# First row tile's attention scores by one 256-column matmul per component, in heads 0 to 5 of a decoder block

## The chip, the cores and the metric

The kernel runs on one core of a Trainium2 chip. The metric is the device time in microseconds (us) of one execution. A core has five engines with instruction queues of their own: PE (matmuls, with its weight loads shown as PEld), DVE (vector operations), ACT (activations and copies), POOL (GpSimd) and SP (which issues most of the transfers). Each queue runs in its own order, and engines wait for one another by semaphores.

## The reference

The block works on 512 rows of width 1024 in float32. Cut to the part around the change:

```python
h = rmsnorm(x, norm_attn_g)
u_q, u_k, u_v, u_pool, u_gate = split(h @ w_in)
# 8 heads, 2 components of 64 dimensions each, values 128 wide
for i in range(S // Q_BLOCK):                 # row tiles of 128
    s = einsum('bqhcd,bkhcd->bhcqk', q[:, q0:kend], k[:, :kend])
    s = where(mask, s, -inf)                  # causal
    p = softmax(s, axis=-1)
    w = p[:, :, 0] - lam * p[:, :, 1]         # difference of the two components
    outs.append(einsum('bhqk,bkhd->bqhd', w, v[:, :kend]))
a = rmsnorm(o, subln_g) * (1 - lam_init)
merged = sigmoid(g_A) * a + sigmoid(g_P) * pool(u_pool)
x = x + merged @ w_out
x = x + relu(rmsnorm(x) @ w_up)**2 @ w_down
```

Queries carry a factor of 1/8, and a rotary embedding turns 16 of the 64 dimensions of queries and keys.

## The kernel before

Precision is kept by splitting operands into a high part in float32r (a reduced float32 format of the matmul) and a low part, the rest. A projection is 24 matmuls of 512 columns: high by high, high by low, low by high (lines 131, 132, 135). For the scores both parts of the query lie one above the other in the 128 partitions: tile `qs` holds, for component 0, the high part in partitions 0 to 63 and the low part in 64 to 127, and the other way round for component 1. The keys are in two tiles. `kz` has the high part against the query's high part and zeros in the other half. `ks` has the low part against the query's high part, and the high part against the query's low part. So a score tile is the sum of two matmuls into one PSUM bank, query by `ks` (line 395, which starts the sum) and query by `kz` (line 396, which ends it), with the same stationary `qs`.

For each head `attn` goes through four row tiles i = 0 to 3 with N = 128(i+1) key columns, and two components c in each. Per tile and component there are the two matmuls of N columns; one DVE reduction (line 397), which adds the causal mask, writes the negated scaled scores to `pr` and takes their row minimum into `st`; and one exponential on ACT (line 401). Then the tile's two components are joined (lines 403 to 406), transposed by PE against the identity (line 410, i+1 transposes), and split into high and low by ACT and DVE (412, 413). After the fourth tile twelve matmuls (line 418) multiply by the values.

Score banks come from a rotation of two, `sbk` = banks 3 and 4: before, each component of a tile takes the next one. Transposes rotate over banks 5 and 6, projections and the merge (lines 485 to 489) over 0 to 2, and bank 7 holds the head's output.

The head loop writes `attn(h)`, the next head's query and key projections `qk(h+1)`, and fillers (a pooling group's projection, or a gate's) up to a count in the table `LAG`. This isn't the order in which engines run. The tile framework's scheduler, with a timeline of its own, interleaves the instructions of these pieces on each engine when the program is built. So an edit of a few instructions gives another order in the whole attention stage. Transfers and all stages outside attention keep their code.

Of the kernel before, what the change touches and what calls it, by code (L numbers as in the profile page):

```python
# [18 lines left out]
P = 128  # L19
# [32 lines left out]
def block_kernel(ctx, tc, xT, x_tok, gains, pos, consts, w_in, w_v, w_pool, w_out, w_up, w_dn, out):  # L52
# [37 lines left out]
    def f(ap):  # L90
        return ap.bitcast(F32)
# [270 lines left out]

    lo_, hi_ = slice(0, 64), slice(64, 128)

    kzs = [cf.tile([P, 2, S], F32R, name=f"kz{i}") for i in range(2)]
    for kz in kzs:
        G.memset(f(kz)[hi_, 0, :], 0.0)
        G.memset(f(kz)[lo_, 1, :], 0.0)

    def qk(h):  # L370
        qs = tp.tile([P, 2, S], F32R, tag="qs", name=f"qs{h}", bufs=2)
        ks = tp.tile([P, 2, S], F32R, tag="ks", name=f"ks{h}", bufs=2)
        kz = kzs[h % 2]
        q = rope(proj(h, f"q{h}", V) if h else q0, f"q{h}")
        for c, own, oth in ((0, lo_, hi_), (1, hi_, lo_)):
            A.copy(out=qs[own, c, :], in_=q[own])
            V.tensor_tensor(out=qs[oth, c, :], in0=q[own], in1=f(qs)[own, c, :], op=ALU.subtract)
        k = rope(proj(8 + h, f"k{h}", V), f"k{h}")
        for c, own, oth in ((0, lo_, hi_), (1, hi_, lo_)):
            A.copy(out=kz[own, c, :], in_=k[own])  # L380
        for c, own, oth in ((0, lo_, hi_), (1, hi_, lo_)):
            A.copy(out=ks[oth, c, :], in_=f(kz)[own, c, :])
            V.tensor_tensor(out=ks[own, c, :], in0=k[own], in1=f(kz)[own, c, :], op=ALU.subtract)
        return qs, ks, kz

    def attn(h, qs, ks, kz):
        wt = wt_all
        for i in range(NT):
            N = (i + 1) * P
            qsl = slice(i * P, i * P + P)  # L390
            pr = tmp(f"p{i}", f"p{h}_{i}", (P, 2, N), bufs=1)
            st = tmp("st", f"st{h}_{i}", (P, 6), bufs=3)
            for c in range(2):
                s_ = sbk(f"s{h}_{i}_{c}")
                T.matmul(s_[:, :N], lhsT=qs[:, c, qsl], rhs=ks[:, c, :N], start=True, stop=False)
                T.matmul(s_[:, :N], lhsT=qs[:, c, qsl], rhs=kz[:, c, :N], start=False, stop=True)  # L396
                V.tensor_tensor_reduce(  # L397
                    out=pr[:, c, :N], in0=s_[:, :N], in1=mask[:, S - N :], scale=-0.125, scalar=-NEG,
                    op0=ALU.add, op1=ALU.min, accum_out=st[:, c : c + 1],
                )  # L400
                A.activation(out=pr[:, c, :N], in_=pr[:, c, :N], func=AF.Exp, scale=-1.0,  # L401
                             bias=st[:, c : c + 1], accum_out=st[:, 2 + c : 3 + c])
            V.reciprocal(out=st[:, 4:6], in_=st[:, 2:4])
            V.tensor_scalar(out=st[:, 5:6], in0=st[:, 5:6], scalar1=lvec, scalar2=None, op0=ALU.mult)
            A.activation(out=pr[:, 1, :N], in_=pr[:, 1, :N], func=AF.Copy, scale=st[:, 5:6])
            V.scalar_tensor_tensor(out=pr[:, 0, :N], in0=pr[:, 0, :N], scalar=st[:, 4:5], in1=pr[:, 1, :N],
                                   op0=ALU.mult, op1=ALU.add)
            t_ = tbk(f"t{h}_{i}")
            for j in range(i + 1):
                T.transpose(out=t_[:, j * P : j * P + P], in_=pr[:, 0, j * P : j * P + P], identity=ident)  # L410
            tv = t_[:, :N].rearrange("p (j q) -> p j q", q=P)
            A.copy(out=wt[:, 0, : i + 1, qsl], in_=tv)
            V.tensor_tensor(out=wt[:, 1, : i + 1, qsl], in0=tv, in1=f(wt)[:, 0, : i + 1, qsl], op=ALU.subtract)
        o_ = obk(f"o{h}")
        n = 0
        for vv, ww in ((vh, 0), (vl, 0), (vh, 1)):
            for j in range(NT):
                T.matmul(o_[:, j * P :], lhsT=vv[:, h, j * P : j * P + P], rhs=wt[:, ww, j, j * P :], start=n == 0, stop=n == 11,  # L418
                         skip_group_check=True)
                n += 1  # L420
        o = tmp("o", f"o{h}", bufs=2)
        A.copy(out=o, in_=o_)
        sqh = tmp("sqh", f"sqh{h}", dt=F32R, bufs=1)
        A.activation(out=sqh, in_=o_, func=AF.Square)
        sql = tmp("y", f"sql{h}", dt=F32R, bufs=1)
        sq = tmp("sq", f"sqo{h}")
        (V if h == H - 1 else G).tensor_tensor(out=sq, in0=o, in1=o, op=ALU.mult)
        (V if h == H - 1 else G).tensor_tensor(out=sql, in0=sq, in1=f(sqh), op=ALU.subtract)
        ss = obk(f"ss{h}")
        T.matmul(ss, lhsT=onesr, rhs=sqh, start=True, stop=False)  # L430
        T.matmul(ss, lhsT=onesr, rhs=sql, start=False, stop=True)
        y = tmp("y", f"y{h}", bufs=1)
        rsqrt(y, ss, sq, P)
        if h == H - 1:
            return o, y
        V.scalar_tensor_tensor(out=o, in0=o, scalar=subc, in1=y, op0=ALU.mult, op1=ALU.mult)
        return o, None
# [594 lines left out]
```

## Time and profile before

| | us |
|---|---|
| median of three runs (674.47 to 674.83) | 674.77 |
| the profiled execution's own time | 674.09 |
| its span, first to last instruction | 671.9 |
| PE busy | 663.1 (99%) |
| weight loads (beside PE) | 579.6 (86%) |
| DVE busy | 526.1 (78%) |
| ACT busy | 461.0 (69%) |
| POOL busy | 112.0 (17%) |

The mean granted PE clock was 0.996. The profiled execution's time is 2.19 us above its span, and 0.68 us below the median of the runs. Attention, with the projections and the merges that run among it, fills about 70 to 300 us of the span. In timelines the columns are start in us, duration in us, engine, line, operation, output and inputs, shapes, and a count; an entry in brackets is the idle time ahead of the instruction and what ended it. A matmul's duration reaches from its start until it leaves the array, and the next starts long before that; what a matmul costs PE is the step from its start to the next one's.

### The profile page before, as it was taken

What the parts mean: (1) busy time and instruction counts of PE and PEld (TensorE: products, weight loads), DVE (VectorE), ACT (ScalarE), POOL (GpSimd) and SP (SyncE); (2) the same over time, 40 slices, a digit from 0 to 9 for tenths busy, and PEclk for the clock granted to TensorE, in tenths of its full rate; (3) what the DMA queues carried; (4) which work ended last, traced back from release to release, by engine and by line L of the source; (5) the groups of instructions that cost most, each with busy time, mean ns of one, the idle gap of its engine ahead of it and who ended that gap; (6) DMA issues with size and microseconds to landing.
All of it is one profiled execution on the core that took longest, in us unless ns stands there. A gap on an engine that the chain in (4) does not pass through costs nothing.

```text
span 671.9 us, 9994 instructions
## 1 busy us (share of the span) xinstructions
PE 663.1 (99%) x3688; PEld 579.6 (86%) x3688; DVE 526.1 (78%) x882; ACT 461.0 (69%) x741; POOL 112.0 (17%) x130
## 2 busy tenths in 40 slices
PE   9999999999999999999999999999999999999995
PEld 7888888888888888888889988999889998899884
DVE  6855977799979986875588998657994599747995
ACT  8465587978887698884477975367743695256974
POOL 2001110142133212520202020202102021210120
PEclk9999999999999999999999999999999999999998
DMA  9416464435263365574976596776959578494863
GB/s 317 162 57 185 126 151 126 103 94 126 87 142 103 98 166 105 126 184 172 312 208 112 159 235 186 167 191 146 236 199 187 193 164 261 117 212 132 214 126 125
DMA packets 32880, 109.34 MB, mean 163 GB/s; under 512 B 4032, under 2 KB 4928, under 8 KB 32832
## 3 DMA queue, kind: packets, MB, share of 16 engines
q0 software_dynamic: 10656, 38.80, 32.3%
q1 hardware_dynamic: 21744, 69.38, 29.3%
q8 instruction: 29, 0.48, 0.3%
q10 hardware_dynamic: 432, 0.52, 0.2%
q14 instruction: 19, 0.16, 0.1%
HBM read 106.59 MB, written 2.10 MB: 162 GB/s over the span
## 4 chain that ended last, share of the span: by engine, by line
PE 98%; DMA 1%; DVE 0%; ACT 0%; issue 0%; SPq 0%
PE um L785 8%; PE um L788 8%; PE um L782 8%; PE dm L875 8%; PE dm L877 8%; PE dm L878 8%; PE v L235 2%; PE o L418 2%; PE ga L132 2%; PE ga L131 2%; PE gp L135 2%; PE gp L132 2%; PE k L132 2%; PE k L131 2%; PE gp L131 2%; PE k L135 2%
## 5 line engine op out<-in xcount | busy, mean ns | idle before, releaser
L877 PE MATMUL dm<-wh_dt,z 128*128 128x512 f32 (+1 forms) x128 | 49.5, 386 | 0.0
L878 PE MATMUL dm<-wl_dt,z 128*128 128x512 f32 (+1 forms) x128 | 49.4, 386 | 0.0
L875 PE MATMUL dm<-wh_dt,z 128*128 128x512 f32 (+1 forms) x128 | 49.0, 387 | 0.0
L785 PE MATMUL um<-gss,wh_ut 128*128 128x256 f32 x192 | 48.2, 283 | 0.0
L782 PE MATMUL um<-gss,wh_ut 128*128 128x256 f32 x192 | 48.0, 283 | 0.0
L401 ACT ACTIVATE p<-p,st 128x128 f32<-128x128 f32 (+3 forms) x64 | 35.7, 558 | 14.1 <-DVE st L397 13.8
L895 DVE TENSOR_TENSOR x<-x,dm 128x512 f32<-128x512 f32 x48 | 32.5, 681 | 16.3 <-PE dm L878 16.3
L112 ACT CAST wh_ut<-wga_uNone 128x1024 fp32r<-128x1024 f32 x24 | 24.9, 1050 | 29.7 <-PE dm L877 19.2
L112 ACT CAST wh_ub<-wr_u 128x1024 fp32r<-128x1024 f32 x24 | 25.1, 1050 | 22.1 <-PE um L785 9.8
L686 POOL DMA_DIRECT2D wga_dNone<-w_dn x16 | 14.2, 885 | 154.2 <-DVE wl_dt L113 154.2
L113 DVE TENSOR_TENSOR wl_ut<-wga_uNone,wh_ut 128x1024 fp32r<-128x1024 f32 x24 | 29.1, 1221 | 13.0 <-ACT wh_ut L112 12.9
L877 PE MATMUL dm<-wh_db,z 128*128 128x512 f32 x96 | 37.2, 389 | 0.0
L878 PE MATMUL dm<-wl_db,z 128*128 128x512 f32 x96 | 37.2, 389 | 0.0
L785 PEld LDWEIGHTS um<-gss,wh_ut 128*128 128x128 f32 x192 | 36.9, 192 | 0.0
L782 PEld LDWEIGHTS um<-gss,wh_ut 128*128 128x128 f32 x192 | 36.8, 192 | 0.0
L875 PE MATMUL dm<-wh_db,z 128*128 128x512 f32 x96 | 35.7, 389 | 0.0
L113 DVE TENSOR_TENSOR wl_ub<-wr_u,wh_ub 128x1024 fp32r<-128x1024 f32 x24 | 29.1, 1219 | 7.4 <-ACT wh_ub L112 7.4
L686 POOL DMA_DIRECT2D wga_uNone<-w_up x18 | 15.6, 865 | 115.8 <-DVE wl_ut L113 81.4
L112 ACT CAST wh_dt<-wga_dNone 128x1024 fp32r<-128x1024 f32 x24 | 24.9, 1049 | 14.4 <-issue 6.7
L755 DVE TENSOR_TENSOR z<-rawz,z 128x1024 fp32r<-128x1024 f32 x28 | 33.6, 1218 | 0.5 <-ACT z L752 0.5
L397 DVE CUSTOM_DVE_ANT_0 p<-s,mask 128x128 f32<-128x128 f32 (+3 forms) x64 | 30.3, 484 | 3.6 <-PE s L396 3.5
L785 PE MATMUL um<-gab,wh_ub 128*128 128x256 f32 x128 | 32.5, 283 | 0.0
(324 smaller groups left out, 2203.3 us busy)
## 6 DMA issues: line engine op xcount, KB each, us to landing
wr_u<-w_up SPq DMA_DIRECT2D x24, 512.0 KB, 5.4
wr_d<-w_dn SPq DMA_DIRECT2D x24, 512.0 KB, 4.2
wga_uNone<-w_up POOLq DMA_DIRECT2D x18, 512.0 KB, 7.2
wga_dNone<-w_dn POOLq DMA_DIRECT2D x16, 512.0 KB, 5.7
wr_k<-w_in SPq DMA_DIRECT2D x8, 512.0 KB, 3.3
wr_ga<-w_in SPq DMA_DIRECT2D x8, 512.0 KB, 3.3
wr_gp<-w_in SPq DMA_DIRECT2D x8, 512.0 KB, 4.2
wl_ga<-w_in POOLq DMA_DIRECT2D x8, 512.0 KB, 5.4
```

The source lines that it names most:

```text
L112: ins = A.copy(out=hi[:, sl], in_=raw[:, sl])
L113: (eng or G).tensor_tensor(out=lo[:, sl], in0=raw[:, sl], in1=f(hi)[:, sl], op=ALU.subtract)
L131: T.matmul(acc, lhsT=hi[:, c], rhs=rh[:, k, :], start=k == 0, stop=False)
L132: T.matmul(acc, lhsT=hi[:, c], rhs=rl[k], start=False, stop=False)
L401: A.activation(out=pr[:, c, :N], in_=pr[:, c, :N], func=AF.Exp, scale=-1.0, bias=st[:, c : c + 1], accum_out=st[:, 2 + c : 3 + c])
L755: lo = V.tensor_tensor(out=z[:, 1], in0=r, in1=f(z[:, 0]), op=ALU.subtract)
L782: m = T.matmul(a_, lhsT=hi[:, c], rhs=rh[:, k, :], start=p + k == 0 and onto is None, stop=False, skip_group_check=True)
L785: T.matmul(a_, lhsT=hi[:, c], rhs=rl[:, k, :], start=False, stop=False, skip_group_check=True)
L788: m = T.matmul(a_, lhsT=lo[:, c], rhs=rh[:, k, :], start=False, stop=k == 3, skip_group_check=True)
L875: m = T.matmul(a_, lhsT=zh, rhs=hi[:, sl], start=p == 0 and start, stop=False, skip_group_check=True)
L877: T.matmul(a_, lhsT=zl, rhs=hi[:, sl], start=False, stop=False, skip_group_check=True)
L878: end = T.matmul(a_, lhsT=zh, rhs=lo[:, sl], start=False, stop=p == 3, skip_group_check=True)
```

## The change

In heads 0 to 5 the first row tile (i = 0, N = 128) has its scores made by one matmul for each component instead of two. `ks` and `kz` become halves of one tile `kk`, so that the first 128 columns of both are one moving operand of 2 x 128 columns. The two partial scores of a component come out side by side in PSUM instead of summed, and both components share one bank, `both`: four blocks of 128 columns. The sum is made on DVE. One new addition (after's line 400) takes the `ks` blocks of both components, 2 x 128 columns, adds the causal mask and writes to `pr`; then the reduction of each component (line 406, in place of 397) takes the `kz` block from PSUM and `pr` in place of the mask. Heads 6 and 7, and all other row tiles, keep two matmuls for each component.

```diff
-    kzs = [cf.tile([P, 2, S], F32R, name=f"kz{i}") for i in range(2)]
+    kks = [cf.tile([P, 2, 2, S], F32R, name=f"kk{i}") for i in range(2)]
...
-        ks = tp.tile([P, 2, S], F32R, tag="ks", name=f"ks{h}", bufs=2)
-        kz = kzs[h % 2]
+        ks, kz = (kks[h % 2][:, i] for i in range(2))
...
+            whole = i == 0 and h < 6
+            if whole:
+
+                both = sbk(f"s{h}_0").rearrange("p (c k n) -> p c k n", c=2, k=2)
+                for c in range(2):
+                    T.matmul(both[:, c], lhsT=qs[:, c, qsl], rhs=kk[:, :, c, :P], start=c == 0, stop=True, skip_group_check=True)
+                diag = mask[:, S - P :].rearrange("p (o n) -> p o n", o=1).to_broadcast([P, 2, P])
+                V.tensor_tensor(out=pr, in0=both[:, :, 0], in1=diag, op=ALU.add)
             for c in range(2):
-                s_ = sbk(f"s{h}_{i}_{c}")
-                T.matmul(s_[:, :N], lhsT=qs[:, c, qsl], rhs=ks[:, c, :N], start=True, stop=False)
-                T.matmul(s_[:, :N], lhsT=qs[:, c, qsl], rhs=kz[:, c, :N], start=False, stop=True)
+                if not whole:
+                    s_ = sbk(f"s{h}_{i}_{c}")
...
-                    out=pr[:, c, :N], in0=s_[:, :N], in1=mask[:, S - N :], scale=-0.125, scalar=-NEG,
+                    out=pr[:, c, :N], in0=both[:, c, 1] if whole else s_[:, :N], in1=pr[:, c] if whole else mask[:, S - N :],
+                    scale=-0.125, scalar=-NEG,
```

In the built program lines behind 385 stand about ten higher, so that 395, 396, 397, 406, 410 and 418 are 404, 405, 406, 416, 420 and 428 after. In the order's rows a name such as `s0_1_0_646` is the score bank of head 0, row tile 1, component 0, and the last number only tells buffers apart; `ga0` is a gate's projection, a filler.

On PE, around head 0's first scores, the order before:

```order
L131 MATMUL ga0_884<-xh_84,wh_ga0_879 128x512
L395 MATMUL s0_0_0_626<-ks0_570,qs0_569 128x128
L396 MATMUL s0_0_0_626<-kz0_563,qs0_569 128x128
L132 MATMUL ga0_884<-xlb_86,wh_ga0_879 128x512
L395 MATMUL s0_0_1_631<-ks0_570,qs0_569 128x128
L396 MATMUL s0_0_1_631<-kz0_563,qs0_569 128x128
L131 MATMUL ga0_884<-xh_84,wh_ga0_879 128x512
```

And after, at the same place:

```order
L131 MATMUL ga0_880<-xh_84,wh_ga0_875 128x512
L398 MATMUL s0_0_625<-kk0_563,qs0_569 128x256
L404 MATMUL s0_1_0_643<-kk0_563,qs0_569 128x256
L405 MATMUL s0_1_0_643<-kk0_563,qs0_569 128x256
L398 MATMUL s0_0_625<-kk0_563,qs0_569 128x256
L132 MATMUL ga0_880<-xlb_86,wh_ga0_875 128x512
```

Two pairs of 128 columns have become two matmuls of 256, and the scores of row tile 1, component 0, which stood 18 rows below head 0's first score matmul, have come up between them: `both` takes one bank of the rotation, so that the other is free at once.

On DVE, at head 0's first reductions, the order before:

```order
L354 TENSOR_TENSOR q1k1_815<-q1k1_815,swk1_817 128x512
L397 ISA p0_0_624,st0_0_625<-s0_0_0_626,mask_96 128x128
L397 ISA st0_0_625 128x1
L457 SCALAR_TENSOR_TENSOR pb0_864<-pa0_863,u0_860 128x512
L397 ISA p0_0_624,st0_0_625<-s0_0_1_631,mask_96 128x128
L397 ISA st0_0_625 128x1
L383 TENSOR_TENSOR ks1_742<-q1k1_815,kz1_564 64x512
```

And after:

```order
L354 TENSOR_TENSOR q1k1_811<-q1k1_811,swk1_813 128x512
L400 TENSOR_TENSOR p0_0_623<-s0_0_625,mask_96 128x256
L467 SCALAR_TENSOR_TENSOR pb0_860<-pa0_859,u0_856 128x512
L406 ISA p0_0_623,st0_0_624<-s0_0_625,p0_0_623 128x128
L406 ISA st0_0_624 128x1
L406 ISA p0_0_623,st0_0_624<-s0_0_625,p0_0_623 128x128
L406 ISA st0_0_624 128x1
L406 ISA p0_1_641,st0_1_642<-s0_1_0_643,mask_96 128x256
L406 ISA st0_1_642 128x1
L382 TENSOR_TENSOR kk1_564<-q1k1_811,kk1_564 64x512
```

The addition stands ahead, both reductions behind it, and row tile 1's first reduction has moved up past the next head's key splits (before's line 383, after's 382).

On PE, around the transposes of head 4's last row tile (`t4_3`), which wait for DVE's join of that tile (line 406 before, 416 after), the order before:

```order
L131 MATMUL q6_2257<-xh_84,wh_q6_2253 128x512
L395 MATMUL s5_0_0_2134<-ks5_1960,qs5_1959 128x128
L396 MATMUL s5_0_0_2134<-kz1_564,qs5_1959 128x128
L132 MATMUL q6_2257<-xla_85,wh_q6_2253 128x512
L131 MATMUL q6_2257<-xh_84,wh_q6_2253 128x512
L132 MATMUL q6_2257<-xla_85,wh_q6_2253 128x512
L131 MATMUL q6_2257<-xh_84,wh_q6_2253 128x512
L132 MATMUL q6_2257<-xlb_86,wh_q6_2253 128x512
L410 MATMUL t4_3_1921<-ident_87,p4_3_1905 128x128 x4
```

And after:

```order
L398 MATMUL s5_0_2118<-kk1_564,qs5_1944 128x256
L404 MATMUL s5_1_0_2136<-kk1_564,qs5_1944 128x256
L405 MATMUL s5_1_0_2136<-kk1_564,qs5_1944 128x256
L132 MATMUL q6_2238<-xla_85,wh_q6_2234 128x512
L398 MATMUL s5_0_2118<-kk1_564,qs5_1944 128x256
L131 MATMUL q6_2238<-xh_84,wh_q6_2234 128x512
L132 MATMUL q6_2238<-xlb_86,wh_q6_2234 128x512
L131 MATMUL q6_2238<-xh_84,wh_q6_2234 128x512
L132 MATMUL q6_2238<-xlb_86,wh_q6_2234 128x512
L131 MATMUL q6_2238<-xh_84,wh_q6_2234 128x512
L420 MATMUL t4_3_1906<-ident_87,p4_3_1890 128x128 x4
```

From head 5's first score matmul to these transposes PE has, before, a pair of 128 columns and five matmuls of 512, and after, four of 256 and six of 512. On DVE, between the second of head 5's key splits and the join that the transposes wait for, there was nothing before, and after there is one operation of 128x512 (line 446, of head 3's output).

SP's order is the same row for row. On POOL the rows are the same and a few stand one to three places elsewhere, among them one accumulating weight transfer of a gate and three multiplications of line 482.

More of the change, by code (lines that the diff above doesn't have):

```diff
@@ L363, in block_kernel @@
     lo_, hi_ = slice(0, 64), slice(64, 128)
-    kzs = [cf.tile([P, 2, S], F32R, name=f"kz{i}") for i in range(2)]
-    for kz in kzs:
-        G.memset(f(kz)[hi_, 0, :], 0.0)
-        G.memset(f(kz)[lo_, 1, :], 0.0)
+    kks = [cf.tile([P, 2, 2, S], F32R, name=f"kk{i}") for i in range(2)]
+    for kk in kks:
+        G.memset(f(kk)[hi_, 1, 0, :], 0.0)
+        G.memset(f(kk)[lo_, 1, 1, :], 0.0)
     def qk(h):
         qs = tp.tile([P, 2, S], F32R, tag="qs", name=f"qs{h}", bufs=2)
-        ks = tp.tile([P, 2, S], F32R, tag="ks", name=f"ks{h}", bufs=2)
-        kz = kzs[h % 2]
+        ks, kz = (kks[h % 2][:, i] for i in range(2))
         q = rope(proj(h, f"q{h}", V) if h else q0, f"q{h}")
@@ L383, in qk, with attn @@
             V.tensor_tensor(out=ks[own, c, :], in0=k[own], in1=f(kz)[own, c, :], op=ALU.subtract)
-        return qs, ks, kz
-    def attn(h, qs, ks, kz):
+        return qs, kks[h % 2]
+    def attn(h, qs, kk):
+        ks, kz = (kk[:, i] for i in range(2))
         wt = wt_all
@@ L392, in attn @@
             st = tmp("st", f"st{h}_{i}", (P, 6), bufs=3)
+            whole = i == 0 and h < 6
[5 more added lines that the diff above has]
+                V.tensor_tensor(out=pr, in0=both[:, :, 0], in1=diag, op=ALU.add)
             for c in range(2):
-                s_ = sbk(f"s{h}_{i}_{c}")
-                T.matmul(s_[:, :N], lhsT=qs[:, c, qsl], rhs=ks[:, c, :N], start=True, stop=False)
-                T.matmul(s_[:, :N], lhsT=qs[:, c, qsl], rhs=kz[:, c, :N], start=False, stop=True)
+                if not whole:
+                    s_ = sbk(f"s{h}_{i}_{c}")
+                    T.matmul(s_[:, :N], lhsT=qs[:, c, qsl], rhs=ks[:, c, :N], start=True, stop=False)
+                    T.matmul(s_[:, :N], lhsT=qs[:, c, qsl], rhs=kz[:, c, :N], start=False, stop=True)
                 V.tensor_tensor_reduce(
-                    out=pr[:, c, :N], in0=s_[:, :N], in1=mask[:, S - N :], scale=-0.125, scalar=-NEG,
+                    out=pr[:, c, :N], in0=both[:, c, 1] if whole else s_[:, :N], in1=pr[:, c] if whole else mask[:, S - N :],
+                    scale=-0.125, scalar=-NEG,
                     op0=ALU.add, op1=ALU.min, accum_out=st[:, c : c + 1],
```

## The prediction

> **What bounds the kernel now.** I read the shares of busy time first, then the chain that ended last, then PE's waits, and then busy time by stretches of the attention stage.
>
> ```profile
> PE 663.1 (99%) x3688; PEld 579.6 (86%) x3688; DVE 526.1 (78%) x882; ACT 461.0 (69%) x741; POOL 112.0 (17%) x130
> PE 98%; DMA 1%; DVE 0%; ACT 0%; issue 0%; SPq 0%
> PEld t L410 <- issue: 0.2, 1, 0.2
> PEld s L395 <- DVE st L397: 0.2, 1, 0.2
> PEld u L131 <- DVE g L474: 0.2, 1, 0.2
> core 0: us, PE busy (x) PEld busy (x) DVE busy (x) ACT busy (x) POOL busy (x), PEclk, DMA share, GB/s
> 60.00:140.00 80.00, 80.00 (x380) 66.81 (x379) 61.30 (x144) 57.50 (x106) 11.38 (x13) 1.00 0.53 131
> 140.00:180.00 40.00, 40.00 (x196) 33.54 (x195) 38.25 (x88) 33.23 (x67) 11.34 (x13) 1.00 0.43 106
> 180.00:200.00 20.00, 20.00 (x102) 16.93 (x101) 15.11 (x37) 16.72 (x29) 6.27 (x5) 1.00 0.58 138
> 200.00:240.00 40.00, 40.00 (x191) 33.14 (x190) 38.69 (x80) 30.22 (x59) 10.98 (x11) 1.00 0.34 94
> 240.00:300.00 60.00, 59.94 (x294) 50.07 (x293) 46.46 (x112) 51.86 (x95) 20.41 (x18) 1.00 0.62 141
> ```
>
> PE carries 98% of the chain, and in the attention stage it is busy all the time: the last five rows, which are windows with their length and each engine's busy time, give 239.94 of 240 us, at full clock (1.00). The three waits of the weight loads are all that PE shows in attention, 0.2 us each. So time is gained here only if PE's own instructions get shorter, and lost only if a new wait opens on PE. Who could open one is DVE: it is busy 38.25 of 40 us from 140 to 180 and 38.69 of 40 from 200 to 240, and idle 1.75 and 1.31 us there. The change takes work from PE and gives work to DVE, in just this stage.
>
> **The PE term.** A busy PE isn't PE at its peak, so I price by steps from start to start in the timeline of PE:
>
> ```profile
> 80.84 0.39 PE L131 MATMUL ga<-xh,wh_ga 128*128 128x512 f32 x1
> 81.07 0.22 PE L395 MATMUL s<-ks,qs 128*128 128x128 f32 x1
> 81.13 0.27 PE L396 MATMUL s<-kz,qs 128*128 128x128 f32 x1
> 81.24 0.45 PE L132 MATMUL ga<-xlb,wh_ga 128*128 128x512 f32 x1
> 81.52 0.22 PE L395 MATMUL s<-ks,qs 128*128 128x128 f32 x1
> 81.58 0.28 PE L396 MATMUL s<-kz,qs 128*128 128x128 f32 x1
> 81.69 0.45 PE L131 MATMUL ga<-xh,wh_ga 128*128 128x512 f32 x1
> 81.98 0.40 PE L132 MATMUL ga<-xlb,wh_ga 128*128 128x512 f32 x1
> ...
> 86.31 0.28 PE L395 MATMUL s<-ks,qs 128*128 128x256 f32 x1
> 86.42 0.28 PE L396 MATMUL s<-kz,qs 128*128 128x256 f32 x1
> 86.54 0.39 PE L131 MATMUL q<-xh,wh_q 128*128 128x512 f32 x1
> 86.77 0.28 PE L395 MATMUL s<-ks,qs 128*128 128x256 f32 x1
> ```
>
> A plain 512 step is 0.23 us (80.84 to 81.07, 86.54 to 86.77). Pair and 512 together take 0.45 (81.07 to 81.52) and 0.46 (81.52 to 81.98), so a pair of 128 columns costs 0.22 to 0.23, of which 0.06 and 0.11 stand on its own two steps, and the rest makes the next step 0.28 or 0.29 instead of 0.23. Two of 256 take 0.23 (86.31 to 86.54), 0.115 each. So 128 columns cost as much as 256: each carries a weight load of its own, and that, not the columns, sets about 0.11. With one matmul of 256 in place of a pair, 0.23 - 0.115 = 0.115 us goes, 12 times (two components, six heads): 1.38 us. By the smaller pair (0.22) it is 1.26.
>
> Nobody shows a 256 alone between two of 512, nor a moving operand in two blocks of 128. Bounds from the rows: 0.06, if it were priced by the short first step (then each place saves 0.17, 2.0 us in all), and 0.23, if two blocks cost two matmuls (saves nothing). I take 0.115, since four rows of that width stand beside it.
>
> A rule that speaks against the change is in the Trainium skill, page "TensorE: Matmul & The Clock Gate", section "Back-to-back issue gap": a warm matmul's isolated step is its columns at 2.4 GHz plus about 2.5 ns, 134 and 262 cycles for 128 and 256 columns. By that two of 128 would cost no less than one of 256 and the term would be about zero. The same page gives a weight load 128 cycles at 1.2 GHz ("LDWEIGHTS"), an estimate of 0.107 us, and with it the trace's 0.22 to 0.23 for a pair agrees.
>
> **The DVE term.** An addition of 2 x 128 columns comes in, six times; the reductions keep their width and PSUM input and have `pr` for the mask, both in SBUF. Nearest rows:
>
> ```profile
> L397 DVE CUSTOM_DVE_ANT_0 p<-s,mask 128x256 f32<-128x256 f32 x16 | 6.5, 419 | 2.7 <-PE s L396 2.7
> L413 DVE TENSOR_TENSOR wt<-t,wt 128x256 fp32r<-128x256 f32 x8 | 3.3, 416 | 1.4 <-ACT wt L412 1.4
> L406 DVE SCALAR_TENSOR_TENSOR p<-p,st 128x256 f32<-128x256 f32 x8 | 4.9, 611 | 1.0 <-ACT p L405 0.9
> 88.14 0.42 DVE L397 CUSTOM_DVE_ANT_0 p<-s,mask 128x256 f32<-128x256 f32 x1
> 88.49 0.08 DVE L397 DVE_READ_ACCUMULATOR2_ANT st<- 128x1 f32 x1
> ```
>
> An addition with one PSUM input of this size lasts 0.42 us (the rows of lines 397 and 413), and the next DVE instruction starts 0.35 after it. Six make 2.1 us, up to 6 x 0.61 = 3.7 by line 406, whose inputs are both in SBUF. I take 2.1. Of DVE's idle time from 60 to 300 us (240 - 199.82, the sum of the five windows, = 40.2) it is a twentieth, and it costs nothing while PE's next need comes later. That cover is thin only in 140 to 180 and 200 to 240, in each of which two heads add 0.7 us together to an engine with 1.75 and 1.31 us of idle time. Were it gone there and everywhere, the 2.1 us would land on PE as later transposes or later scores.
>
> **The moves.** The order is new on PE, DVE and ACT through the stage. One part of it helps: with `both` in one bank, row tile 1's first scores follow at once (the first order above) instead of 5 us later (81.07 against 86.31), so a head's chain of reduction, exponential, join and transpose starts earlier. The other side is the bank: it stays taken through addition and two reductions, and row tile 1's second scores need it; they stand 20 rows further down, some 6 us by the steps, and head 0's addition and two reductions last 0.42 + 2 x 0.28. I cost that at nothing. The four memsets stay four of the same shape, and `kk` takes the room of two `ks` and two `kz`: nothing. SP's transfers keep their rows. On POOL the accumulating gate transfer and the multiplications of line 482 shift by a few places; POOL is busy 60.38 of 240 us, and I cost that at nothing too.
>
> **The sum.** The profiled execution took 674.09 (span 671.9 and 2.19 around it); 674.09 - 1.38 = 672.71. It lies 0.68 below the median of the runs, so against that median the forecast is 674.77 - 1.38 = 673.39, say 673.4. A change of 0.2% is 1.35 us, about what a measurement can tell from none, and the forecast sits right on it.
>
> **Rivals.**
>
> A, the forecast: the PE term lands, new waits stay below half a microsecond. For it speaks that the same scheduler left only 0.6 us of visible waits in this stage. Its own range is 672.9 to 673.9, by 2.0 and 0.9 us saved. Chance 0.46, half on either side of 0.2%.
>
> B, the earlier chains also take away waits that PE has now. Besides the 0.6 us there are late steps such as this one:
>
> ```profile
> 264.26 0.28 PE L395 MATMUL s<-ks,qs 128*128 128x128 f32 x1
> 264.37 0.27 PE L396 MATMUL s<-kz,qs 128*128 128x128 f32 x1
> 264.71 0.50 PE L131 MATMUL u<-xh,wh_u 128*128 128x512 f32 x1
> 265.04 0.40 PE L485 MATMUL pp<-dh,wt 128*128 128x512 f32 x1
> ```
>
> From 264.37 to 265.04 are 0.67 us for a 128 and a 512, 0.34 by the prices above, so 0.33 lost at one wait for DVE. Two such places gone give 1.38 + 0.7 = 2.1 saved: 672.7. Against it: few such places are visible. Chance 0.21.
>
> C, DVE's 2.1 us land on PE in part: half of them leave 1.38 - 1.05 = 0.33 saved, 674.4; all of them make 675.5, which is still within 0.2%. For it speaks DVE's 97% from 200 to 240; against it, that only two of six heads lie there. Chance 0.16.
>
> D, slower. One mechanism: DVE operations that read SBUF twice stretch beside POOL, and in the new order they stand ahead of a transpose that now comes too early.
>
> ```profile
> 211.59 1.74 POOL L482 TENSOR_TENSOR o<-o,g 128x512 f32<-128x512 f32 x1
> 210.65 3.23 DVE L383 TENSOR_TENSOR ks<-q1k,kz 64x512 fp32r<-64x512 f32 x2
> 213.91 1.88 DVE L406 SCALAR_TENSOR_TENSOR p<-p,st 128x512 f32<-128x512 f32 x1
> 261.82 1.40 DVE L383 TENSOR_TENSOR ks<-q1k,kz 64x512 fp32r<-64x512 f32 x2
> 214.59 0.22 PE L395 MATMUL s<-ks,qs 128*128 128x128 f32 x1
> 215.97 0.60 PE L410 MATMUL t<-ident,p 128*128 128x128 f32 x4
> ```
>
> The pair of line 383 takes 3.23 us at 210.65 and 1.40 at 261.82, and the join ends at 213.91 + 1.88 = 215.79, 0.18 us ahead of the transposes that read it. In the third order shown, one DVE operation more stands ahead of that join, and PE has 4 x 0.115 + 6 x 0.23 = 1.84 us to the transposes instead of 215.97 - 214.59 = 1.38. With 0.7 us more on DVE and 0.46 more on PE, the 0.18 of slack becomes a wait of about 0.1. So this place alone costs nothing much. It decides when such waits pass 1.38 + 1.35 = 2.7 us; two joins late by one whole stretch of the key splits each (3.23 - 1.40 = 1.83) make 3.7 - 1.38 = 2.3 lost, 677.1, and at 2.8 of waits it is 676.2. Chance 0.13.
>
> The Trainium skill, page "SBUF — State Buffer", section "Who interferes with whom", has the same rule: a DVE instruction with two SBUF inputs contends with a GpSimd instruction that reads SBUF, one with a single SBUF input doesn't. By it the new addition, with one PSUM input, would cost 2.1 and not 3.7 us; no run so far shows that instruction.
>
> E, nothing is saved on PE: if only the columns counted (a step of 0.06, as from 81.07 to 81.13, for each 128), a pair would cost 0.12 and a 256 0.115, and the time stays 674.8. The late steps behind each pair speak against it. Chance 0.04.
>
> **Range and chances.** Faster by over 0.2% is half of A and all of B, 0.44. Slower is D, 0.13. The rest is the other half of A, C and E, 0.43. The range goes from 672.3, a little under B, to 675.5, where all of DVE's addition lands on PE; it leaves out D and a tail below B.
>
> **What the profile after would show.** Six heads with two 256 matmuls of line 398 at steps of about 0.115, and a 512 behind them at 0.23: the PE term is right. At 0.2 or more each, it is wrong. An addition (line 400) of 0.42 us, six times: the DVE term is right. PE's waits in attention at 0.6 us or less: A or B; new entries on transposes waiting for line 416 or scores waiting for line 406: C or D. DVE's key splits (line 382) above 850 ns in the mean, beside POOL, would go with D. The forecast fails most likely by waits at places that the old trace doesn't have, since the whole order is drawn anew.

## Result, and the profile after

The changed kernel takes 675.98 us (median of 14 runs, 675.59 to 676.59), the kernel before 674.49 beside it: ratio 1.0023, 95% interval 1.0015 to 1.0031, so 1.49 us slower where 1.4 faster was forecast. The profiled execution took 675.59 with a span of 673.8, 1.9 more than before.

From its page, the shares of busy time and the chain that ended last; then PE's weight-load waits from 60 to 300 us (total, times, longest), and three of the windows shown in the prediction:

```profile
PE 663.7 (99%) x3676; PEld 578.0 (86%) x3676; DVE 529.4 (79%) x888; ACT 458.6 (68%) x741; POOL 110.9 (16%) x130
PE 86%; DVE 7%; ACT 4%; issue 1%; POOL 1%; DMA 0%; SPq 0%; DVEq 0%; ACTq 0%; POOLq 0%
```

```profile
PEld s L404 <- ACT wh_ga L120: 0.8, 1, 0.8
PEld t L420 <- DVE p L416: 0.7, 2, 0.5
PEld t L420 <- issue: 0.6, 2, 0.3
PEld s L404 <- DVE st L406: 0.2, 1, 0.2
```

```profile
140.00:180.00 40.00, 39.99 (x192) 32.77 (x191) 37.80 (x81) 29.41 (x61) 12.46 (x14) 1.00 0.42 95
200.00:240.00 40.00, 39.97 (x188) 32.83 (x187) 37.36 (x81) 28.19 (x56) 10.84 (x11) 1.00 0.43 118
240.00:300.00 60.00, 59.30 (x287) 49.01 (x286) 48.31 (x113) 52.06 (x98) 20.10 (x18) 1.00 0.59 130
```

PE carries 86% of the chain where it carried 98%, and 11% of it now runs through DVE and ACT. Transposes wait for joins and scores for reductions, and PE has 0.7 us of plain idle time from 240 to 300. In the other windows the busy share hides the waits (39.99 and 39.97 of 40 us), since the ends of matmuls are modelled.

Therefore I count PE's **lost time**: the time between matmul starts less what the steps cost undisturbed, 0.2285 us for 512 columns, 0.172 for 384, 0.115 for 256 and 0.1125 for 128 (so 0.225 a pair), over all matmuls from 60 us on. For the kernel before it is 0.90 us up to 300 us, for the changed one 3.30: 2.40 more, against 12 x (0.225 - 0.115) = 1.32 saved. (The sums themselves hang on these prices; the difference does so only through those of 128 and 256 columns, since all else is the same in both kernels.) That makes +1.08, and read directly, from the first matmul of head 1's `q` (57.17 us before) to the output product's second half (322.59), the changed kernel needs 1.07 us more. The loss lies mainly in three places:

| lost time, us | 60-170 | 170-206 | 206-240 | 240-256 | 256-272 | 272-300 | sum |
|---|---|---|---|---|---|---|---|
| before | 0.20 | 0.06 | 0.16 | 0.10 | 0.33 | 0.05 | 0.90 |
| after | 0.86 | 0.21 | 0.44 | 0.07 | 1.64 | 0.10 | 3.30 |

The largest place is 256 to 272, where heads 6 and 7 have no edit. In the timeline of the changed kernel, first DVE, then PE:

```profile
259.40 2.48 DVE L382 TENSOR_TENSOR kk<-q1k,kk 64x512 fp32r<-64x512 f32 x2
262.89 0.68 DVE L406 CUSTOM_DVE_ANT_0 p<-s,mask 128x512 f32<-128x512 f32 x1
263.50 0.69 DVE L406 CUSTOM_DVE_ANT_0 p<-s,mask 128x512 f32<-128x512 f32 x1
264.14 0.62 DVE L416 SCALAR_TENSOR_TENSOR p<-p,st 128x384 f32<-128x384 f32 x1
...
262.49 0.39 PE L405 MATMUL s<-kk,qs 128*128 128x512 f32 x1
262.96 0.39 PE L441 MATMUL ss<-sql,onesr 128*128 128x512 f32 x1
263.73 0.30 PE L404 MATMUL s<-kk,qs 128*128 128x128 f32 x1 [0.39 <-ACT wh_ga L120]
264.34 0.30 PE L404 MATMUL s<-kk,qs 128*128 128x128 f32 x1 [0.20 <-DVE st L406]
264.82 0.55 PE L420 MATMUL t<-ident,p 128*128 128x128 f32 x3
```

Head 7's two first scores start 0.15 us behind the ends of the two reductions of head 6's last row tile (263.57 and 264.19), which free their banks, and the transposes 0.06 behind the end of the join (264.76). The profile puts the first of these waits down to ACT's copy of a weight (`wh_ga`), which ends just then, at 263.59; run e13 below, where that copy ends 0.66 us ahead of the same score, shows that it isn't what PE waits for. Before, 3.7 us of other matmuls stood between these scores and head 6's (260.33 to 264.01); here it is 0.5.

A last piece lies at the very end. From the transfers of the changed kernel, and of the kernel before, the one of the output that ACT issues (count, size, median us to landing):

```profile
out<-x ACTq DMA_DIRECT2D x1, 256.0 KB, 3.7
```

```profile
out<-x ACTq DMA_DIRECT2D x1, 256.0 KB, 2.8
```

It is the last thing to land, and the span ends 5.0 us behind its issue instead of 4.1, 0.9 more. (SP's last transfer of the output, issued at the same moment, lands in 3.4 us instead of 2.5 as well.) In the two profiled executions the span's 1.9 us are 0.30 less at the start, 1.07 in attention, 0.27 between 349 and 391 us, which no other run of this order shows, and 0.9 at the end. Attention and end make 2.0; the medians of the times say 1.49, with 1.0 to 2.1 by the interval. Most of what is missing lies outside the span: over all executions the time is 2.2 us above the span in the kernel before and 1.8 in the changed kernel. What makes these 0.4 us is open.

### The profile page after: what moved, and what is told of

The parts are those of the page before. It is cut to its first block, busy times and chain, and to the rows that moved or that the text cites. A ratio compares the mean times of both kernels' runs of the same rounds, so it can differ in the third digit from the quotient of the medians.

```text
span 673.8 us, 9974 instructions
## 1 busy us (share of the span) xinstructions
PE 663.7 (99%) x3676; PEld 578.0 (86%) x3676; DVE 529.4 (79%) x888; ACT 458.6 (68%) x741; POOL 110.9 (16%) x130
## 4 chain that ended last, share of the span: by engine, by line
PE 86%; DVE 7%; ACT 4%; issue 1%; POOL 1%; DMA 0%; SPq 0%; DVEq 0%; ACTq 0%; POOLq 0%
PE um L792 8%; PE um L795 8%; PE um L798 8%; PE dm L885 7%; PE dm L887 7%; PE dm L888 7%; PE v L235 2%; PE po L593 2%; PE v L237 2%; PE po L592 2%; PE v L236 2%; PE po L594 2%; PE ga L131 2%; PE gp L132 2%; PE ga L132 2%; PE gp L131 2%
## 5 line engine op out<-in xcount | busy, mean ns | idle before, releaser
L795 PE MATMUL um<-gab,wh_ub 128*128 128x256 f32 x128 | 32.5, 283 | 0.0
L792 PE MATMUL um<-gab,wh_ub 128*128 128x256 f32 x128 | 32.4, 283 | 0.0
```

The costliest lines, as they stand in the source:

```text
L792: m = T.matmul(a_, lhsT=hi[:, c], rhs=rh[:, k, :], start=p + k == 0 and onto is None, stop=False, skip_group_check=True)
L795: T.matmul(a_, lhsT=hi[:, c], rhs=rl[:, k, :], start=False, stop=False, skip_group_check=True)
```

## Experiments

Where an order was given, the drawn order was replaced by a table of instructions for PE, DVE, ACT and POOL, through dependencies that add no wait on a semaphore. The table seems to cost nothing by itself: e3a, in the order of the changed kernel, has that kernel's lost time and shift, and e3b, in the old order, those of the kernel before, though POOL does less in both.

```diff
+    for runs_ in PIN.values():
+        order_ = [named[f"I-{o}"] for a, n in runs_ for o in range(a, a + n)]
+        for x_, y_ in zip(order_, order_[1:]):
+            tc.add_manual_dep(y_, x_.name, mybir.DependencyInfo(mybir.DependencyClass.NoSync, ...), ...)
```

All runs together. "Shift" is the difference to the kernel before from `q1` to the output product, read from the traces; "landing" is that of the last transfer; the last two columns are medians against the kernel before on the same chip. Those intervals are 0.6 us wide to either side; the shift is free of the start's jitter (0.4 us earlier to 0.8 later among these runs). Shift and landing together lie above the medians by 0.3 us on average. That is the time outside the span: 2.2 us in the kernel before, e7, e10 and e3b, and 1.75 to 2.0 in all other runs.

| run | heads edited, order, other change | lost, 60-300 | shift | landing | us over before | ratio (95%) |
|---|---|---|---|---|---|---|
| after | 6, drawn | 3.30 | +1.07 | 3.7 | +1.49 | 1.0023 (1.0015-1.0031) |
| e1 | 6, old | 2.13 | -0.10 | 3.7 | +0.69 | 1.0009 (1.0000-1.0018) |
| e2 | pairs, no addition, after's | 1.75 | +0.85 | 2.8 | +0.62 | 1.0010 (1.0001-1.0019) |
| e6 | 6, after's, no addition | 2.45 | +0.25 | 2.8 | -0.07 | 1.0000 (0.9991-1.0009) |
| e5 | 8, old | 2.42 | -0.24 | 2.8 | -0.39 | 0.9993 (0.9984-1.0001) |
| e7 | 6, old, no addition | 1.52 | -0.69 | 2.8 | -0.74 | 0.9988 (0.9979-0.9997) |
| e9 | 8, old + move | 1.37 | -1.18 | 2.8 | -1.59 | 0.9973 (0.9964-0.9982) |
| e10 | none, old + move | 0.76 | -0.13 | 2.8 | -0.06 | 0.9998 (0.9989-1.0007) |
| e12 | 6, old + move | 1.25 | -0.97 | 3.7 | -0.39 | 0.9996 (0.9987-1.0004) |
| e3a | 6, after's, head 5's POOL squares cut | 3.30 | +1.07 | 3.7 | +1.68 | 1.0023 (1.0014-1.0032) |
| e11 | 6, after's but for head 6 | 3.51 | +1.28 | 3.7 | +1.71 | 1.0026 (1.0016-1.0036) |
| e13 | 6, after's, head 7's rotation cut | 2.85 | +0.63 | 3.7 | +1.04 | 1.0017 (1.0007-1.0026) |
| e3 | 6, after's, POOL cut | 1.81 | -0.41 | 3.7 | +0.19 | 1.0004 (0.9995-1.0013) |
| e3b | none, old, POOL cut | 0.90 | -0.01 | 2.8 | -0.08 | 1.0000 (0.9992-1.0009) |
| e4a | 8, drawn | 3.69 | +1.02 | 2.8 | +0.43 | 1.0011 (1.0002-1.0019) |
| e4b | 4, drawn | 3.46 | +1.66 | 2.8 | +1.39 | 1.0026 (1.0016-1.0037) |
| e14 | as after, 2 idle DVE instructions | 3.23 | +1.01 | 2.8 | +0.63 | 1.0010 (1.0001-1.0018) |
| e15 | none, old, 6 idle DVE instructions | 1.12 | +0.22 | 2.9 | -0.28 | 0.9997 (0.9988-1.0006) |
| e16 | as e12, 2 idle DVE instructions | 1.36 | -0.82 | 2.8 | -1.17 | 0.9983 (0.9974-0.9992) |

### Edit or order (e1, e2, e6, e5)

My first theory: the edit gains its 1.3 us, and the newly drawn order loses more. The rival: the addition, and the bank it holds, make PE wait. e1 and e5 put the edit into the old order (one 256 for each pair, the addition with both reductions at the second reduction's place); e2 puts pairs into the new order, all in one bank; e6 takes only the additions out of the changed kernel.

```diff
 e2
-T.matmul(both[:, c], lhsT=qs[:, c, qsl], rhs=kk[:, :, c, :P], start=c == 0, stop=True, ...)
+for n in range(2):
+    T.matmul(both[:, c, 0], lhsT=qs[:, c, qsl], rhs=(ks, kz)[n][:, c, :P], start=c + n == 0, stop=n == 1, ...)
 e2 and e6 (reductions then take both[:, c, 0] and the mask)
-V.tensor_tensor(out=pr, in0=both[:, :, 0], in1=diag, op=ALU.add)
```

> The instructions of the changed kernel, issued in the order of the kernel before on PE, DVE, ACT and POOL; where a pair of 128 stood, one 256 stands, and the addition stands with both first reductions where the second reduction stood. Theory 1 (the edit saves its 1.35 us, the newly drawn order loses more than twice that): 1.3 us under the kernel before, 673.1 to 673.3, and PE's lost time from 60 to 300 us stays at the 0.9 us of the kernel before. Theory 2 (the addition on DVE, and the bank that it holds, are themselves what PE waits for): lost time of 2 us or more, 674.5 to 676. Theory 3 (the 0.22% are nothing of this stage): no forecast, between the two.

> The order of the changed kernel on PE, DVE, ACT and POOL, but the arithmetic of the kernel before: four matmuls of 128 columns for the first tile, summed in the one bank, and no addition on DVE. Theory 1 (the order loses 2.4 us by itself): the loss stays and the saving goes, 676.5 to 677.3, so 2.0 to 2.8 over the kernel before. Theory 2 (the addition makes the loss): loss gone and no saving, 674.5 to 675.

> The changed kernel in its own order without the six additions on DVE; the reductions take the first block and the mask, so the second block of the scores of the first tile is computed and left out of the result. Theory 1: the waits stay within 0.5 us, since 0.7 us for two heads is little beside splits of the key that stretch by 1 to 4 us: 675.5 to 676, 1.0 to 1.5 over the kernel before. Theory 2: the 2.4 us go with the additions, 673.1 to 673.8.

> The edit in all eight heads, in the order of the kernel before, as in the run with six heads. Theory 1: 16 x 0.115 = 1.84 us saved, 672.6 to 672.9, unless the addition makes a wait in heads 6 and 7, where transposes and joins of DVE lie closest (up to 0.5 us back). Theory 2: slower than the run with six heads by the waits of two more additions, 674.5 to 676.5.

Neither theory holds alone. The order costs 0.85 without addition or saving (e2, 1.75 - 0.90; +0.62 measured, where 2.0 to 2.8 was expected). The additions cost 0.85 in the new order (3.30 - 2.45, e6). With eight heads in the old order the kernel is 0.39 under the kernel before, where the first theory expected 1.6 to 1.9 and the second no gain (e5). And in the old order PE loses 1.2 us as well (e1), 1.0 of it at one place, the transposes of head 4's last row tile. DVE, then PE there in e1:

```profile
211.02 3.24 DVE L390 TENSOR_TENSOR kk<-q1k,kk 64x512 fp32r<-64x512 f32 x2
214.29 1.87 DVE L424 SCALAR_TENSOR_TENSOR p<-p,st 128x512 f32<-128x512 f32 x1
...
215.14 0.39 PE L140 MATMUL q<-xlb,wh_q 128*128 128x512 f32 x1
216.31 0.63 PE L428 MATMUL t<-ident,p 128*128 128x128 f32 x4 [0.78 <-DVE p L424]
```

The splits and the join last what they lasted before (3.23 and 1.88). Counted from `q1`, they stand where they stood (0.06 us earlier), while PE is ready for the transposes 1.04 earlier. PE's saving of heads 0 to 4 ends in this wait.

### What holds the join (e7, e9, e10, e12)

> As the run of the edit in the order of the kernel before (six heads), without the six additions: the reductions take the first block and the mask, and the second block of the scores of the first tile is left out of the result. What is to be told apart is the wait of 0.78 us of head 4's last transposes for the join. Theory A (the additions make DVE late there): the wait goes or stays under 0.2, and the time is 1.2 to 1.4 us under the kernel before. Theory B (DVE's own chain sets that join, with 0.18 us of slack in the kernel before, and what PE saves in heads 0 to 4 cannot pass it): the wait stays at 0.6 to 0.9, and the time is 0.4 to 0.7 under. Between them, if DVE follows PE part of the way: 0.3 to 0.5 of wait.

Without the additions the wait is 0.32, not 0.78, and the lost time 1.52, not 2.13:

```profile
213.43 1.88 DVE L422 SCALAR_TENSOR_TENSOR p<-p,st 128x512 f32<-128x512 f32 x1
215.46 0.63 PE L426 MATMUL t<-ident,p 128*128 128x128 f32 x4 [0.32 <-DVE p L422]
```

So it is between the two: 0.6 by the additions, and 0.4 because DVE's own chain follows PE only part of the way. If DVE and its stretch set the place, a DVE operation moved out of the way should free the saving. One that nobody needs soon is the third window's `u`, which also starts a POOL sum beside the key splits:

```diff
 DVE, lines of e9
-L463 u2<-u2,rb
 L454 o3<-o3,con,y3
 L390 kk<-q1k5,kk  (two key splits)
 L424 p4_3<-p4_3,st4_3
+L463 u2<-u2,rb
 POOL
-L471 pa2<-u2
 L500 o3<-o3,g
 L130 wl_gp4<-w_in
+L471 pa2<-u2
```

> The edit in eight heads in the order of the kernel before, and at the place of head 4's last transposes one move: DVE multiplies the third window's u behind the join and not ahead of the key splits, and POOL's first window sum stands behind its gate product. The key splits and the join then run without the window sum beside them. If DVE and its stretch beside POOL set that place: the splits take 1.4 to 2.6 us for two instead of 3.2, the join starts 0.7 to 1.8 earlier, the wait of 0.8 is gone, and the time is 0.8 to 1.1 under the same edit without the move, 1.1 to 1.5 under the kernel before. If the wait only moves on to the next transposes: no more than 0.3 under the run without the move.

> The kernel before with that one move alone (u of the third window behind the join, the window sum behind the gate product), no edit. PE has only 0.18 us less than a wait there, so an earlier join is worth nothing: within 0.3 us of the kernel before by either theory. A gain of 0.5 or more would say that the move helps somewhere else, and that the run with the edit and the move has its gain from there.

> The edit as it was made, heads 0 to 5, in the order of the kernel before with the one move (u of the third window behind the join, its first window sum behind the gate product). Theory (DVE's chain at head 4's last transposes is what held the saving back): no wait there, PE's lost time at 300 us 1.0 to 1.3 us as in the kernel before, time 0.9 to 1.3 us under the kernel before; the runs with eight heads and the move came out 1.6 under, and two heads are worth 0.46. Rival (the gain of that run is the eight heads): within 0.4 us of the kernel before.

In e9, DVE, POOL and PE:

```profile
210.26 2.38 DVE L390 TENSOR_TENSOR kk<-q1k,kk 64x512 fp32r<-64x512 f32 x2
212.69 0.75 DVE L424 SCALAR_TENSOR_TENSOR p<-p,st 128x512 f32<-128x512 f32 x1
...
210.42 1.67 POOL L500 TENSOR_TENSOR o<-o,g 128x512 f32<-128x512 f32 x1 [10.91 <-DVE o L454]
214.14 1.03 POOL L471 TENSOR_TENSOR pa<-u 128x512 f32<-128x512 f32 x1 [1.21 <-DVE u L463]
...
214.96 0.39 PE L140 MATMUL q<-xlb,wh_q 128*128 128x512 f32 x1
215.19 0.60 PE L428 MATMUL t<-ident,p 128*128 128x128 f32 x4
```

The splits take 2.38 instead of 3.24, the join 0.75 instead of 1.87, and the transposes follow the last 512 at a plain step of 0.23. The same move is worth nothing without the edit (e10, 0.9998), and 0.9 to 1.2 us with it (e5 to e9: shift -0.24 to -1.18, medians -0.39 to -1.59). e12, held against e1, shows the same (shift -0.10 to -0.97, medians +0.69 to -0.39); that its median is only 0.39 under the kernel before comes from the last transfer, below. e9 is the fastest of all, 3.1 us under the changed kernel when each is held against the kernel before (-1.59 and +1.49).

### What the drawn order lacks (e3a, e11, e13, e3, e3b)

> The changed kernel in its own order, with POOL's two operations on head 5's squares (the square and the difference) cut to 16 of 512 columns, so head 5's norm is not that of the reference. They run beside the key splits of head 7 at 258 to 261. Theory: these splits (2.48 us for two) go back to 1.4, and PE's lost time from 256 to 270, 1.65 us, falls to 0.6 or less: 0.8 to 1.2 us under the changed kernel, 0.2 to 0.6 over the kernel before. Rival (in the new order transposes and scores stand too early there, whatever POOL does): the loss stays over 1.3, and the time is that of the changed kernel, 1.3 to 1.6 over the kernel before.

```diff
-G.tensor_tensor(out=sq, in0=o, in1=o, op=ALU.mult)
-G.tensor_tensor(out=sql, in0=sq, in1=f(sqh), op=ALU.subtract)
+G.tensor_tensor(out=sq[:, :16], in0=o[:, :16], in1=o[:, :16], op=ALU.mult)        # e3a: head 5; e3, e3b: heads 0 to 6
+G.tensor_tensor(out=sql[:, :16], in0=sq[:, :16], in1=f(sqh)[:, :16], op=ALU.subtract)
 # e3 and e3b also
-G.tensor_tensor(out=a, in0=a, in1=sa, op=ALU.mult)
+G.tensor_tensor(out=a[:, :16], in0=a[:, :16], in1=sa[:, :16], op=ALU.mult)
```

(PE's matmul of the difference reads the 16 columns 32 times, so that its work stays.) The theory fails: the splits do go back to 1.40 (from 259.86), and nothing is gained, since a DVE operation ahead of the reductions then waits 1.14 us for ACT:

```profile
259.86 1.40 DVE L390 TENSOR_TENSOR kk<-q1k,kk 64x512 fp32r<-64x512 f32 x2
263.01 0.42 DVE L431 TENSOR_TENSOR wt<-t,wt 128x256 fp32r<-128x256 f32 x1 [1.14 <-ACT wt L430]
```

> The changed kernel in its own order, except for one stretch that the edit does not touch: head 6's row tiles 1 to 3, between its first scores and head 7's first scores, go in the order of the kernel before on PE, DVE, ACT and POOL. Theory (the new order puts head 6's scores late against the plain matmuls, so that 0.5 us of PE work is left between s6_3 and s7_0 where 3.7 were): PE's lost time from 256 to 270 us falls from 1.6 us to 0.3 to 0.5, the time is 1.1 to 1.3 us under the changed kernel, 0.2 to 0.6 over the kernel before. Rival (the loss comes from what heads 0 to 5 left behind, PE being early there whatever the order): the loss stays over 1.2 and the time at 1.3 to 1.6 over the kernel before.

The loss from 256 to 272 falls to 0.43 as expected, and yet the kernel is no faster: 1.51 us are lost from 240 to 256 instead. In e11, PE's wait there:

```profile
PE t L428 <- DVE p L424: 1.1, 1, 1.1
```

With head 6 in its old place PE meets head 5's last join, which starts 2.6 us later in the new order than in the old (counted from `q1`). So head 6's place was not the only thing wrong.

> The changed kernel in its own order, with DVE's two rotation operations on head 7's q and k (the product and the sum, four instructions of 0.69 us between 249 and 258 us) cut to 16 of 512 columns, so head 7's rotation is not that of the reference; PE, ACT and POOL do the same work. If DVE's chain is what PE waits for at 258 to 266: DVE is 2.2 us earlier there, PE's lost time from 256 to 270 falls from 1.6 us to 0.6 or less, time 0.2 to 0.6 over the kernel before. If it is ACT's chain, or the two banks of the scores (s6_3 and head 7's first scores 0.5 us of PE work apart): 1.2 or more stays lost, time 1.2 to 1.6 over.

```diff
-V.tensor_tensor(out=sw, in0=sw, in1=sinR, op=ALU.mult)
-V.tensor_tensor(out=q1, in0=q1, in1=sw, op=ALU.add)
+V.tensor_tensor(out=sw[:, :16], in0=sw[:, :16], in1=sinR[:, :16], op=ALU.mult)       # q7 and k7
+V.tensor_tensor(out=q1[:, :16], in0=q1[:, :16], in1=sw[:, :16], op=ALU.add)
```

DVE, ACT and PE in e13:

```profile
262.86 0.69 DVE L415 CUSTOM_DVE_ANT_0 p<-s,mask 128x512 f32<-128x512 f32 x1 [0.43 <-PE s L414]
263.48 0.69 DVE L415 CUSTOM_DVE_ANT_0 p<-s,mask 128x512 f32<-128x512 f32 x1
...
262.00 1.05 ACT L128 CAST wh_ga<-wr_ga 128x1024 fp32r<-128x1024 f32 x1
...
263.71 0.30 PE L413 MATMUL s<-kk,qs 128*128 128x128 f32 x1
264.32 0.30 PE L413 MATMUL s<-kk,qs 128*128 128x128 f32 x1 [0.20 <-DVE st L415]
```

Now DVE waits for head 6's scores before it reduces them, and 1.17 of the 1.64 us stay lost (expected: 0.6 or less, or 1.2 and more; it is the second within 0.03, and 0.45 went). ACT's copy of `wh_ga` ends at 263.05 here, 0.66 us ahead of head 7's first score, and that score still starts 0.16 behind the end of the reduction (263.55): the reductions hold it, not ACT. With DVE early, what is left is the distance in PE's order: two reductions of 0.6 must end before head 7's scores get their two banks. e2 (1.19) and e3 (1.18) end at the same figure by other reliefs. So 0.85 here (1.18 - 0.33) is the order's own, and 0.45 is DVE's lateness.

> The changed kernel in its own order, with three of POOL's operations per head (the square, its difference, the gate product) cut to 16 of 512 columns in all heads but the last, so norm and gate are not those of the reference; POOL's window sums stay. If DVE's stretch beside POOL makes a good part of the 2.4 us of new waits, those of 150 to 164 and 222 to 234 above all: 0.5 to 1.1 us of them go, time 0.4 to 1.0 over the kernel before. If POOL has no part in it, as at 258 to 266 in the run with head 5's squares cut: within 0.2 us of the changed kernel, 1.3 to 1.6 over.

> The kernel before in its own order with the same three operations of POOL cut in the same way: what POOL's work costs there, to hold against the same cut in the changed kernel. PE lost only 0.9 us in all from 60 to 300, so no more than 0.3 us is to be had: 0.0 to 0.4 under the kernel before. More than 0.6 would say that the cut helps in a way that has nothing to do with the edit.

This is the run that shows what makes DVE late. The changed kernel, DVE then POOL, ahead of head 2's last transposes, and DVE in e3:

```profile
144.60 4.98 DVE L382 TENSOR_TENSOR kk<-q1k,kk 64x512 fp32r<-64x512 f32 x2
153.20 1.78 DVE L416 SCALAR_TENSOR_TENSOR p<-p,st 128x512 f32<-128x512 f32 x1
...
144.82 1.51 POOL L492 TENSOR_TENSOR o<-o,g 128x512 f32<-128x512 f32 x1
146.06 1.26 POOL L463 TENSOR_TENSOR pb<-pa 128x512 f32<-128x512 f32 x1
147.06 1.25 POOL L437 TENSOR_TENSOR sqo<-o 128x512 f32<-128x512 f32 x1
152.72 1.72 POOL L438 TENSOR_TENSOR sql<-sqo,sqh 128x512 fp32r<-128x512 f32 x1
```

```profile
145.07 2.66 DVE L390 TENSOR_TENSOR kk<-q1k,kk 64x512 fp32r<-64x512 f32 x2
151.34 0.74 DVE L424 SCALAR_TENSOR_TENSOR p<-p,st 128x512 f32<-128x512 f32 x1
```

With three POOL operations per head cut, the lost time falls by 1.49 us, from 0.86 to 0.22 before 170, from 0.44 to 0.11 at 206 to 240, and from 1.64 to 1.18 at 256 to 272; the same cut in the kernel before moves nothing (0.90 and 0.90). Without the additions (e6) the loss at the first two places falls as well, to 0.42 and 0.14. So DVE is late there by both together, and either relief takes most of it; their prices do not add. With the order's own 0.85 the 1.49 make 2.34 of the 2.40.

### Other drawings (e4a, e4b), and the last transfer (e14 to e16)

```diff
-            whole = i == 0 and h < 6
+            whole = i == 0 and h < 8      # e4a; e4b: h < 4
```

> The edit in all eight heads with no order given: the order is drawn anew. If each drawing has late steps at places of its own: 1.84 us saved on PE and waits between 0.7 and 3.2 us, so anything from 673.1 to 675.7, with the losses at other places than with six heads. If the loss belongs to the edit and grows with its heads: 1.5 to 2.2 over the kernel before.

> The edit in heads 0 to 3 alone, order drawn anew. If each drawing has late steps of its own: 0.92 us saved on PE and waits between 0.7 and 3.2 us, from 0.2 under to 2.3 over the kernel before, at other places than with six heads. If the loss belongs to the edit and grows with its heads: 0.9 to 1.1 over the kernel before.

The losses over the kernel before are 2.56, 2.40 and 2.79 us for four, six and eight heads, so they don't grow with the edit as the saving does (0.88, 1.32, 1.76). Against my expectation they lie in the same places: before 170 (0.85 or 0.86 in all three) and at 256 to 272 (2.1 and 2.2 for eight and four heads); only the piece from 206 to 240 is missing with four heads (0.14). So the drawn orders are alike. The old order with eight heads (e5) loses 1.27 us less than the drawn one, without any move, and its median is 0.82 better.

```diff
+            nop = cf.tile([P, 2], F32, name="nop")
+            for i in range(2):            # e14, e16; e15: 6
+                V.tensor_tensor(out=nop[:, :1], in0=mask[:, :1], in1=mask[:, :1], op=ALU.add)
```

> The changed kernel in its own order with two tiny DVE additions (one column, result used nowhere) behind head 0's first addition: 890 DVE instructions and not 888. The last output transfer, issued by ACT, took 3.7 us to land in each of the seven kernels with the edit and its additions in six heads, in whatever order, and 2.8 to 3.2 in the ten others. If that hangs on how long the engines' programs are and not on the work: it lands in 2.8 to 3.2, and the time is 0.7 to 0.9 us under the changed kernel, 0.5 to 0.9 over the kernel before. If it hangs on the edit: 3.7 again and no change.

> The kernel before with six of these tiny DVE additions, so 888 DVE instructions. If the number of DVE instructions sets the landing of the last transfer: 3.7 us in place of 2.8, and 0.7 to 0.9 us over the kernel before. If not: 2.8, and within 0.3 us of the kernel before; the six stand where DVE has idle time.

> The edit in six heads in the order of the kernel before with the one move (which came out at 0.9996 of the kernel before, its last transfer landing in 3.7 us), with two tiny DVE additions. If the program's length sets the landing: 2.8 to 3.2 us, and 0.9 to 1.3 us under the kernel before. If not: again 0.2 to 0.5 under.

Two instructions of no use make the changed kernel 0.9 us better against the kernel before (+1.49 to +0.63) and e12 0.8 better (-0.39 to -1.17), with the shifts 0.06 less and 0.15 more. In both the transfer of ACT lands in 2.8 us again, as in the kernel before. So these 0.9 us don't belong to the edit's work. The number of DVE instructions alone doesn't decide it either: e15 has 888 as the changed kernel has, and lands in 2.9. What about the program does is open.

## Why the prediction was wrong

**The PE term** was right. From the changed kernel's instructions of line 398 (count, ns min/median/max, first and last start), and its timeline of PE:

```profile
L398 PE MATMUL s<-kk,qs x12: 277/278/284, 80.8 to 215.0; 128*128 128x256 f32 x12
```

```profile
149.79 0.28 PE L405 MATMUL s<-kk,qs 128*128 128x256 f32 x1
149.91 0.28 PE L398 MATMUL s<-kk,qs 128*128 128x256 f32 x1
150.03 0.40 PE L132 MATMUL q<-xla,wh_q 128*128 128x512 f32 x1
```

A step of 0.12, as the 256 of one block beside it, and not the 0.22 of a pair. With 0.11 us saved for each pair, lost and saved time give the shift within 0.11 us in every run of the table. The Trainium skill, page "TensorE: Matmul & The Clock Gate", section "Back-to-back issue gap", gives 134 and 262 cycles for an isolated matmul of 128 and 256 columns, by which a pair would cost about as much as one of 256 (the prediction's "no less" says it the wrong way round); the same section says that in a stream with weight loads both set the spacing. The trace agrees with the second: each matmul here has a weight load of its own, and a pair costs 0.225 against 0.115 to 0.12.

**The DVE term** had the right duration and the wrong cover:

```profile
L400 DVE TENSOR_TENSOR p<-s,mask x6: 408/412/417, 81.9 to 219.7; 128x256 f32<-128x256 f32 x6
```

The 2.1 us forecast were to cost nothing while PE's next need comes later; they cost 0.85 of lost time in the drawn order (e6) and 0.61 in the old one (e7). That is rival C's "in part".

**The moves** are the step that failed: "I cost that at nothing" stood behind the new order, POOL's shifts among it. The order costs 0.85 by itself at heads 6 and 7, and the stretch beside POOL, together with the additions, 1.49. Rival D named this mechanism and gave it 0.13. Its place, head 4's last transposes, was wrong for the changed kernel, where the join ends at 215.11 and they start at 216.31 without a wait, and right for the edit in the old order (0.78 of wait in e1). Its price, more than 2.7 of waits, was near but not reached: 2.40. Waits and saving alone make 1.08, or 0.16%; that the kernel came out slower by over 0.2% is owed to the last transfer, which no rival had. The Trainium skill's page "SBUF — State Buffer", section "Who interferes with whom", says that a DVE instruction with two SBUF inputs contends with a POOL instruction that reads SBUF, and one with a single SBUF input doesn't. The trace agrees: the splits and joins, with two SBUF inputs, go from 2.48 to 1.40 and 1.78 to 0.74 as POOL's work is cut, while the reductions of 128x384 (line 406), which read PSUM and SBUF, last 0.54 to 0.56 in the changed kernel, six of them beside POOL as well as the ten others. Of the addition itself no run shows it: it lasts 0.41 to 0.42, and none of the six ran beside POOL.

The row that should have changed the sum was in the prediction: the join at head 4 ended 0.18 us ahead of PE. I used it only to price an extra DVE operation. It also says how much earlier PE may come before it waits: 0.18, where heads 0 to 4 save about 1.0. My working at that place, a wait of about 0.1, counted PE's way from head 5's first scores and left out that PE already gets there about 1.0 us earlier. Even 0.18 was too much: in e1 and e7 these transposes start 0.15 behind the end of the join.

A and B fell with it. Forecast and measurement lie 2.9 us apart: 2.40 of waits, 0.06 of the PE term (1.32 for 1.38) and 0.9 of the last transfer, less 0.4 outside the span. The time of 675.98 is 0.5 above the range. Without the 0.9, which nobody could have read from the profile before, it would have been inside (e14: 674.90, 0.63 over the kernel before), but by luck: it would still have been slower where the forecast said faster. A slip in the range of A changed nothing: with 2.0 saved its lower end is 672.8 and not 672.9.

## What to carry over

When PE is busy 99% of the time, look at how long each input was ready before PE used it: a saving can stop at the smallest such slack, and passes further only if the producer comes earlier too (of 1.32 us saved, 0.10 passed in e1, 0.69 without the additions in e7 and 0.97 with the move in e12). Before costing a redrawn order at nothing, hold the old order and make the edit in it; then relieve the one handoff that waits (here one DVE operation and one POOL sum moved, worth nothing alone and 0.9 to 1.2 us with the edit).

## What the runs showed of the hardware

The last output transfer lands in 3.7 us in the changed kernel and six other runs with its edit and additions in six heads, and in 2.8 to 2.9 in the kernel before and all others, among them e14 and e16, which carry the same edit and two idle DVE instructions. The time outside the span differs between programs too, 2.2 us in the kernel before and 1.8 in the changed kernel. A difference of 0.1% between two programs can be these alone, so both are worth a look before a small loss is explained by the edit. What sets them no run here shows.
